# The sigmoid of a projected group, issued later by a fiber of its own, in the last block of a hybrid decoder layer's input projection

## The chip, the cores and the metric

The kernel runs on one core of a Trainium2 chip. The engines of that core work through queues of their own, each in order: PE (TensorE, matrix products into PSUM), DVE (VectorE), ACT (ScalarE), POOL (GpSimd) and SP (SyncE, which here issues the transfers from memory). They wait for each other through semaphores. The metric is the time of one execution in microseconds (us), lower is better; several executions are timed and their median is given.

## The reference

The layer takes x (256 tokens of 4096 channels) and a condition vector c. Cut to what matters here:

```python
mod = c @ w_ada + b_ada                       # shift, scale, gate: 3 x 4096
u = x * (1.0 + scale) + shift
proj = u @ w_in                               # 4096 -> 11824 columns
(rg_x, rg_g, nsa_q, kv_c, kv_s, kv_w, nsa_gl, nsa_g,
 hg_q, hg_f, hg_i, hg_g) = split(proj)
y_rg  = rg_lru(conv(rg_x)) * silu(rg_g)       # gated linear recurrence
y_nsa = nsa(nsa_q, kv_c, kv_s, kv_w, nsa_gl) * silu(nsa_g)   # sparse attention
y_hg  = hgrn2(silu(hg_q), hg_f, hg_i) * silu(hg_g)           # chunked recurrence
y = concat([y_rg, y_nsa, y_hg]) @ w_out
x = layer_norm(ALPHA * x + (1.0 + gate) * y)
```

silu(a) is a * sigmoid(a). Four of the twelve parts pass through it: rg_g, hg_q, hg_g and nsa_g, together 20 groups of 256 columns. All is float32.

## The kernel before, in words

**The projection.** w_in is read once, in ten blocks of rows (KB gives their sizes; the last five are 4 x 128 rows each). A block is walked as a row of steps, one for about 1024 columns of weights in SBUF: in the last block a step is mostly one group of 256 output columns, 24 matmuls. The groups come in the order of GROUPS: kc, vc, four rg_g, four rg_x, four hg_q, four hg_g, hg_f and hg_i in turn, ks, one nsa_q, kw, vw, eight nsa_g, seven nsa_q, vs. Each group has a sum `acc` in SBUF (ACC) over the ten blocks.

**A step.** Weights are split in a rounded part `hi` and a remainder `lo`, so that three fast matmuls make one float32 product. `split` issues, three steps ahead of the matmuls, on ACT the casts `hi` (1024 wide) and `ps` (a second copy of half of it in PSUM), on POOL one half of `lo`, on DVE the other half. There are four raw, four hi and four lo buffers. In program order a step is: the split of the step three further on; the loads; the first half of the matmuls; `post` of the step before (which empties PSUM: DVE adds `mm` to `acc`); one turn of the background work; the second half of the matmuls; another turn of the background work; then `ease` and `ada_loads`, which issue on DVE the sums of a chunk of the gate matrix w_ada (two instructions `ps<-ra,pk,ps`). The line L119 that most profile rows show is the helper through which DVE, ACT and POOL instructions are issued, so rows are told apart by their tiles.

**The last block.** Here `post` does more (the lines inside `if kb == NKB - 1`): for a group in SILU it issues at once, behind the DVE addition, a sigmoid on ACT into a buffer `ev` (two buffers) and a multiplication of `acc` by `ev` on POOL; then the group is entered in `done`. Between the last block's steps stand 16 steps of another kind (cmp), which compress keys and values: a few small matmuls each on weights `ra` from w1, and no split.

**Background work.** The three head groups are generators ("fibers") on lanes: rg_fiber, hg_fiber, nsa_fiber. They start when the groups they need are in `done` and buffers suffice. `run_bg` makes a turn: it counts one tick, gives every entry of the list `fibers` a go, then every lane. `advance` lets a fiber run to its next yield if its due tick has come, and sets the next due tick from what the planner thinks the engines owe. That estimate is the class Meter: each engine has a ledger `owed`, to which an instruction adds a fixed part and a part per column (DVE 0.06 + 0.00104 per column, ACT 0.09 + 0.00084, POOL 0.16 + 0.0021; ACT also 1.3 when the function table changes), and from which 1.28 (HALF) is taken in each turn. In the last block a step has two turns. Lanes stand still while the ledger of DVE or ACT is over 2.5 (MAY_OWE); the list `fibers` doesn't. An rg_fiber uses sigmoid and tanh, then exp, then sqrt, and so changes ACT's function table on its way; an hg_fiber uses sigmoid, and sqrt near its end.

The order of the program is thus fixed when the kernel is built, and each engine follows its own part of it.

Of the kernel before, what the change touches and what calls it, by code (L numbers as in the profile page):

```python
# [11 lines left out]
FT = mybir.dt.float32  # L12
FR = mybir.dt.float32r
I32 = mybir.dt.int32
AF = mybir.ActivationFunctionType
# [3 lines left out]
P = 128  # L19
# [37 lines left out]
def chunks(kb):  # L57

    n, out, cur, o = KB[kb], [], [], 0
    for g in GROUPS:  # L60
        m = max(1, min(n, 1024 // g[3]))
        for a in range(0, n, m):
            b = min(n, a + m)
            if o + (b - a) * g[3] > 1024:
                out.append((cur, o))
                cur, o = [], 0
            cur.append((g, a, b, o))
            o += (b - a) * g[3]
    out.append((cur, o))
    return out  # L70
# [64 lines left out]
def trunk(ctx: ExitStack, tc: tile.TileContext, pack, xT, xz, w_ada, b_row, w_in, w_out, rg_w, w1, w2,  # L135
          ln_gb, out):
    nc = tc.nc
    dve = Meter(nc.vector, 0.06, 0.00104)
    act = Meter(nc.scalar, 0.09, 0.00084)
    pool = Meter(nc.gpsimd, 0.16, 0.0021)  # L140
# [3 lines left out]
    strm = ctx.enter_context(tc.tile_pool(name="strm", bufs=1))  # L144
# [7 lines left out]
    def nm(s):  # L152
        cnt[0] += 1
        return f"{s}_{cnt[0]}"
# [6 lines left out]
    def slot(name, shape, dt=FT):  # L161
        used[0] += 1
        return ring.tile(shape, dt, name=nm(name), tag="slot", bufs=NRING)

    def ps_mm():
        return psum.tile([P, 512], FT, name=nm("mm"), tag="ps", bufs=8)
# [177 lines left out]
    cur, tick = [0], [0]  # L344
# [78 lines left out]
    ACC = {}  # L423
    done = set()
# [3 lines left out]
    for kb in range(NKB):  # L428
        state = {}
        for items, width in chunks(kb):  # L430
            st = Step("win", off, width)
            st.kb = kb
            off += P * width
            steps.append(st)
            for g, a, b, o in items:

                def mm(st=st, g=g, a=a, b=b, o=o, kb=kb, state=state):
                    name, i, _, w, lay = g
                    k0 = KB0[kb] + a
                    hi, lo = (t_[:, o:o + (b - a) * w].rearrange("p (k w) -> p k w", w=w) for t_ in (st.hi, st.lo))  # L440
                    if a == 0:
                        state[name, i] = [ps_mm() for _ in range(2 if w > 256 else 1)]
                    ps = state[name, i]
                    for j in range(2):
                        dst = ps[j][:, :w] if w > 256 else ps[0][:, j * 256:(j + 1) * 256]
                        for k in range(b - a):
                            uh, ul = U[k0 + k]
                            s, e = a + k == 0, a + k == KB[kb] - 1
                            if lay == "nt":
                                wh, wl = hi[:, k, j * P:(j + 1) * P], lo[:, k, j * P:(j + 1) * P]  # L450
                                seq = ((wh, uh), (wh, ul), (wl, uh))
                            else:
                                wh, wl = hi[:, k], lo[:, k]
                                uh, ul = uh[:, j * P:(j + 1) * P], ul[:, j * P:(j + 1) * P]
                                seq = ((uh, wh), (uh, wl), (ul, wh))
                            for n_, (l_, r_) in enumerate(seq):
                                nc.tensor.matmul(dst, lhsT=l_, rhs=r_, start=s and n_ == 0, stop=e and n_ == 2)  # L457
                        yield

                def post(g=g, b=b, kb=kb, state=state):  # L460
                    if b < KB[kb]:
                        return
                    name, i, _, w, _ = g
                    key = (name, i)
                    ps = state.pop(key)
                    if kb == 0:
                        ACC[key] = slot("acc", [P, 2, 256])
                    acc = ACC[key]
                    if w > 256:
                        pairs = [(x_, ps[j][:, c0:c1]) for j in range(2)  # L470
                                 for x_, c0, c1 in ((acc[:, j], 0, 256), (gl[:, j], 256, 304))]
                    else:
                        pairs = [(acc.rearrange("p a b -> p (a b)"), ps[0])]
                    n_post[0] += 1
                    for x_, p_ in pairs:
                        if kb == 0:
                            act.copy(x_, p_)
                        elif w == 256 and n_post[0] % EVAC[KB[kb]] == EVAC[KB[kb]] - 1:
                            t_ = strm.tile([P, 512], FT, name=nm("ev"), tag="ev", bufs=2)
                            act.copy(t_, p_)  # L480
                            pool.tensor_add(x_, t_, x_)
                        else:
                            dve.tensor_add(x_, p_, x_)
                    if kb == NKB - 1:
                        if name in SILU:
                            t_ = strm.tile([P, 2, 256], FT, name=nm("ev"), tag="ev", bufs=2)
                            act.activation(t_, acc, AF.Sigmoid)
                            pool.tensor_mul(acc, acc, t_)
                        done.add(key)

                st.work.append((mm, post))
    n_win = len(steps)
    first_of = {}
    for i, st in enumerate(steps):
# [5 lines left out]
    def cmp_step(which, c):  # L500
# [21 lines left out]
        def post():  # L522
# [11 lines left out]
            done.add(("cmp_h", which))  # L534

        st.work.append((mm, post))
        return st

# [409 lines left out]
    for pi, part in enumerate(PARTS):  # L948
        for nb in range(NB):
            state = {}  # L950
            for ci, pr in enumerate(part):
# [26 lines left out]
                def post(x, pi=pi, nb=nb, ci=ci, state=state, part=part, between=None):  # L978
# [22 lines left out]
                    else:  # L1001
                        dve.tensor_add(z, ps, z)

                st.work.append((mm, post))
                wout_steps.append(st)

# [58 lines left out]
    fibers = []  # L1065
# [265 lines left out]
HALF = 1.28  # L1331
AFTER = (0.2, 1.5)
# [70 lines left out]
```

## Time and profile before

| what | value |
|---|---|
| median of 3 runs | 1662.71 us (1659.02 to 1663.55) |
| the profiled execution's own time | 1660.88 us |
| its span, from first to last instruction | 1659.1 us |
| PE busy, share of the span | 1597.9 us, 96% |
| DVE | 1331.8 us, 80% |
| ACT | 971.6 us, 59% |
| POOL | 954.5 us, 58% |
| mean granted clock of PE | 0.99 |

The shares are averages over the whole span; the last block of the projection lies between about 955 and 1170 us. The first of the 20 sigmoids starts at 966.69 us and the last at 1133.33 us.

### The profile page before, as it was taken

The page shows a single profiled execution, that of the slowest core. Times are in us where ns is not written, and L with a number is a line of the kernel's source. Part 1 is how long each engine was busy: PE and PEld are TensorE (multiplying, and loading weights), DVE is VectorE, ACT ScalarE, POOL GpSimd, SP SyncE. Part 2 cuts the span into 40 slices and gives each one's busy share as a digit, 9 for nine tenths or more (in the row PEclk, how much of TensorE's full clock was granted, in tenths as well). Part 3 has the DMA queues.
Part 4 walks back from the last instruction along what each step waited for, and adds up shares of the span by engine and source line. Part 5 has one row for each costly group of instructions (what it writes and reads, how often), then busy time and mean ns, then how long its engine had stood idle before and what let it go on. Part 6 is the DMA issues. An engine that isn't in the chain of part 4 may idle for free.

```text
span 1659.1 us, 33161 instructions
## 1 busy us (share of the span) xinstructions
PE 1597.9 (96%) x11752; PEld 1497.6 (90%) x11752; DVE 1331.8 (80%) x2301; ACT 971.6 (59%) x1557; POOL 954.5 (58%) x765
## 2 busy tenths in 40 slices
PE   4999999999999999999999999889999999999997
PEld 4999999998999999999999998889888888878884
DVE  5668978799788788788787797899689688968875
ACT  2887666665655555555555566763565566656562
POOL 1579987776655455555455446576453445455655
PEclk9999999999999999999999998999999999999998
DMA  7998989999999899899899886767667766689983
GB/s 287 368 344 313 365 292 343 309 370 327 328 351 334 289 347 327 299 351 327 303 333 332 312 300 223 247 230 266 230 230 242 238 204 215 222 296 374 338 318 126
DMA packets 146486, 491.49 MB, mean 296 GB/s; under 512 B 16264, under 2 KB 17288, under 8 KB 146320
## 3 DMA queue, kind: packets, MB, share of 16 engines
q1 hardware_dynamic: 146320, 489.38, 82.5%
q8 instruction: 92, 1.51, 0.4%
q14 instruction: 74, 0.61, 0.1%
HBM read 485.12 MB, written 4.19 MB: 295 GB/s over the span
## 4 chain that ended last, share of the span: by engine, by line
PE 79%; DVE 11%; DMA 3%; issue 3%; ACT 3%; POOL 0%; SPq 0%; DVEq 0%; ACTq 0%
PE mm L457 50%; PE mm L969 21%; DVE ps L119 3%; DVE acc L119 2%; DVE lo L119 2%; DMA ra<-in_w_ada_dram 1%; ACT hi L119 1%; DMA raw<-in_w_in_dram 1%; PE ps L708 1%; DVE rgt L119 1%; PE ps L901 1%; PE ps L1287 1%; DVE rgy L119 1%; PE ps L792 1%; PE ps L395 1%
## 5 line engine op out<-in xcount | busy, mean ns | idle before, releaser
L119 POOL TENSOR_TENSOR lo<-raw,hi 128x576 fp32r<-128x576 f32 (+4 forms) x527 | 707.7, 1344 | 609.3 <-ACT hi L119 588.4
L119 ACT CAST hi<-raw 128x1024 fp32r<-128x1024 f32 (+3 forms) x527 | 529.1, 1004 | 487.3 <-POOL lo L119 220.4
L457 PE MATMUL mm<-uh,hi 128*128 128x256 f32 x2560 | 719.3, 281 | 15.3 <-DVE lo L119 9.2
L457 PE MATMUL mm<-uh,lo 128*128 128x256 f32 x2560 | 714.0, 279 | 1.9 <-DVE lo L119 1.4
L457 PE MATMUL mm<-ul,hi 128*128 128x256 f32 x2560 | 713.6, 279 | 0.0
L119 DVE SCALAR_TENSOR_TENSOR ps<-ra,pk,ps 128x512 f32<-128x512 f32 x744 | 520.8, 728 | 8.7 <-DMA ra<-in_w_ada_dram 2.9
L457 PEld LDWEIGHTS mm<-uh,hi 128*128 128x128 f32 x2560 | 485.3, 190 | 19.0 <-DVE lo L119 11.8
L457 PEld LDWEIGHTS mm<-uh,lo 128*128 128x128 f32 x2560 | 485.1, 189 | 2.6 <-DVE lo L119 1.9
L457 PEld LDWEIGHTS mm<-ul,hi 128*128 128x128 f32 x2560 | 485.6, 190 | 0.3 <-issue 0.2
L119 DVE TENSOR_TENSOR lo<-raw,ps 128x448 fp32r<-128x448 f32 (+4 forms) x500 | 303.2, 607 | 224.3 <-ACT ps L119 182.6
L119 ACT CAST ps<-raw 128x448 fp32r<-128x448 f32 (+4 forms) x500 | 259.5, 519 | 7.2 <-DVE acc L119 6.5
L119 DVE TENSOR_TENSOR acc<-mm,acc 128x512 f32<-128x512 f32 (+1 forms) x346 | 231.5, 670 | 0.0
L969 PE MATMUL mm<-hi,yh 128*128 128x512 f32 x512 | 210.8, 412 | 0.3 <-ACT ev L119 0.3
L969 PE MATMUL mm<-hi,yl 128*128 128x512 f32 x512 | 201.3, 393 | 0.0
L969 PE MATMUL mm<-lo,yh 128*128 128x512 f32 x512 | 200.1, 391 | 0.0
L969 PEld LDWEIGHTS mm<-hi,yh 128*128 128x128 f32 x512 | 96.4, 188 | 23.4 <-issue 5.7
L969 PEld LDWEIGHTS mm<-hi,yl 128*128 128x128 f32 x512 | 96.1, 188 | 21.6
L457 PE MATMUL mm<-hi,uh 128*128 128x256 f32 (+1 forms) x384 | 110.6, 288 | 4.9 <-ACT hi L119 3.0
L969 PEld LDWEIGHTS mm<-lo,yh 128*128 128x128 f32 x512 | 96.5, 188 | 19.1 <-issue 1.2
L457 PE MATMUL mm<-lo,uh 128*128 128x256 f32 (+1 forms) x384 | 108.9, 284 | 0.0
L457 PE MATMUL mm<-hi,ul 128*128 128x256 f32 (+1 forms) x384 | 108.9, 284 | 0.0
L119 POOL TENSOR_TENSOR acc<-ev,acc 128x512 f32<-128x512 f32 x77 | 101.2, 1315 | 2.8 <-ACT ev L119 2.5
(193 smaller groups left out, 1480.0 us busy)
## 6 DMA issues: line engine op xcount, KB each, us to landing
ra<-in_w_ada_dram SPq DMA_DIRECT2D x323, 512.0 KB, 5.8
raw<-in_w_in_dram SPq DMA_DIRECT2D x291, 512.0 KB, 5.1
raw<-in_w_out_dram SPq DMA_DIRECT2D x128, 512.0 KB, 4.6
raw<-in_w_in_dram SPq DMA_DIRECT2D x90, 384.0 KB, 5.2
ra<-in_w_ada_dram SPq DMA_DIRECT2D x64, 384.0 KB, 5.5
ra<-in_w_dram SPq DMA_DIRECT2D x16, 512.0 KB, 3.9
raw<-in_w_ada_dram SPq DMA_DIRECT2D x13, 512.0 KB, 5.6
xz<-in_xz_dram SPq DMA_DIRECT2D x16, 256.0 KB, 6.0
```

The costliest lines, as they stand in the source:

```text
L119: return f(*a, **k)
L395: nc.tensor.matmul(pp[:, q:q + 1], lhsT=acc[q], rhs=ones[:, 0:1], start=kb > 0, stop=True, skip_group_check=kb == 0)
L457: nc.tensor.matmul(dst, lhsT=l_, rhs=r_, start=s and n_ == 0, stop=e and n_ == 2)
L708: nc.tensor.matmul(pl[:, (2 * x + j) * 64:(2 * x + j + 1) * 64], lhsT=k[:, j, x * P:(x + 1) * P], rhs=qp[:, j, x * P:(x + 1) * P].rearrang ...
L792: nc.tensor.matmul(s1[:, b * T:(b + 1) * T], lhsT=q[:, j, P:], rhs=kk[b][:, g], start=True, stop=True)
L901: nc.tensor.matmul(o, lhsT=v0, rhs=eT[:, 0:2], start=b == 0, stop=False)
L969: nc.tensor.matmul(state[x], lhsT=a_, rhs=b_, start=ci == 0 and j == 0 and n_ == 0, stop=ci == len(part) - 1 and j == 1 and n_ == 2)
L1287: nc.tensor.matmul(pb, lhsT=rows[-1 - x], rhs=rows[i // 2][:, i % 2 * 512:i % 2 * 512 + 512], start=True, stop=True)
```

## The change

The branch for groups in SILU no longer issues the sigmoid and the multiplication itself. It puts a new generator `silu(key)` on the list `fibers`, with a due tick that depends on the ledgers of DVE and POOL at that moment. When its tick has come, the fiber issues the same two instructions on the same tiles and enters the group in `done`. AFTER[1] is 1.5. Groups outside SILU are entered in `done` at once, as before.

```diff
                     if kb == NKB - 1:
                         if name in SILU:
-                            t_ = strm.tile([P, 2, 256], FT, name=nm("ev"), tag="ev", bufs=2)
-                            act.activation(t_, acc, AF.Sigmoid)
-                            pool.tensor_mul(acc, acc, t_)
-                        done.add(key)
+                            owed = max(dve.owed, pool.owed)
+                            fibers.append([silu(key), 0, 0, 0, tick[0] + 1 + math.ceil((owed + AFTER[1]) / HALF)])
+                        else:
+                            done.add(key)
 
                 st.work.append((mm, post))
+    def silu(key):
+
+        acc = ACC[key]
+        t_ = strm.tile([P, 2, 256], FT, name=nm("ev"), tag="ev", bufs=2)
+        act.activation(t_, acc, AF.Sigmoid)
+        pool.tensor_mul(acc, acc, t_)
+        done.add(key)
+        yield 0
+
```

## Rows read from the trace of the kernel before

**Rows 1.** The page: busy time and share; the chain that ended last, by engine.
```profile
PE 1597.9 (96%) x11752; PEld 1497.6 (90%) x11752; DVE 1331.8 (80%) x2301; ACT 971.6 (59%) x1557; POOL 954.5 (58%) x765
...
PE 79%; DVE 11%; DMA 3%; issue 3%; ACT 3%; POOL 0%; SPq 0%; DVEq 0%; ACTq 0%
```

**Rows 2.** Busy time of each engine in four stretches.
```profile
core 0: us, PE busy (x) PEld busy (x) DVE busy (x) ACT busy (x) POOL busy (x), PEclk, DMA share, GB/s
961.00:1012.00 51.00, 50.77 (x425) 50.03 (x425) 40.67 (x64) 36.35 (x56) 27.03 (x21) 1.00 0.78 277
1012.00:1021.00 9.00, 6.94 (x34) 6.74 (x34) 6.79 (x11) 4.82 (x7) 3.32 (x3) 0.63 0.61 215
1021.00:1060.00 39.00, 32.41 (x229) 30.43 (x228) 38.41 (x54) 19.37 (x32) 25.80 (x19) 0.91 0.68 240
1085.00:1141.00 56.00, 49.27 (x402) 47.75 (x401) 55.46 (x86) 29.75 (x46) 45.36 (x38) 0.97 0.72 248
```

**Rows 3.** The chain, 955 to 1160 us, shares by line.
```profile
by line: issue 11.9%; DVE acc L119 11.0%; PE mm L457 8.8%; DVE lo L119 8.6%; DVE ps L119 7.5%; DVE rgt L119 7.4%; DVE rgy L119 6.5%; DVE hgA L119 5.3%; ACT hi L119 4.9%; DVE hgqp L119 3.3%; PE ps L708 3.1%; DMA raw<-in_w_in_dram 2.8%; ACT p
```

**Rows 4.** Waits, 940 to 1200 us: total us, times, longest.
```profile
ACT ev L119 <- DVE acc L119: 41.3, 14, 7.8
POOL acc L119 <- ACT ev L119: 31.0, 15, 8.9
...
ACT L119 <- DVE acc L119: 3.5, 1, 3.5
...
ACT ev L119 <- POOL acc L119: 2.8, 2, 1.4
```

**Rows 5.** DVE groups in 961:1021, then 1021:1060: busy, mean ns, idle before.
```profile
L119 DVE TENSOR_TENSOR lo<-raw,ps 128x512 fp32r<-128x512 f32 x13 | 8.9, 683 | 10.0 <-ACT ps L119 7.8 <-POOL acc L119 2.2
...
L119 DVE TENSOR_TENSOR lo<-raw,ps 128x512 fp32r<-128x512 f32 x9 | 6.1, 680 | 2.0 <-ACT ps L119 2.0
```

**Rows 6.** Timeline of ACT, 994 to 1020 us: start, duration, idle before.
```profile
993.98 0.90 ACT L119 ACTIVATE rgt<-rgr,p 128x256 f32<-128x256 f32 x2
996.18 0.63 ACT L119 ACTIVATE ev<-acc 128x512 f32<-128x512 f32 x1 [1.30 <-DVE acc L119]
...
1004.68 1.28 ACT L119 ACT_TABLE_LOAD   x1
1006.02 0.63 ACT L119 ACTIVATE ev<-acc 128x512 f32<-128x512 f32 x1
1006.55 1.04 ACT L119 CAST hi<-raw 128x1024 fp32r<-128x1024 f32 x1
...
1012.90 0.58 ACT L119 CAST ps<-raw 128x512 fp32r<-128x512 f32 x1
1016.94 1.28 ACT L119 ACT_TABLE_LOAD   x1 [3.46 <-DVE acc L119]
...
1018.77 1.03 ACT L119 CAST hi<-raw 128x1024 fp32r<-128x1024 f32 x1
```

**Rows 7.** Timeline of DVE, 1000 to 1021 us.
```profile
1000.55 0.69 DVE L119 TENSOR_TENSOR lo<-raw,ps 128x512 fp32r<-128x512 f32 x1 [2.94 <-ACT ps L119]
...
1008.10 0.69 DVE L119 TENSOR_TENSOR lo<-raw,ps 128x512 fp32r<-128x512 f32 x1 [2.12 <-ACT ps L119]
...
1020.32 0.69 DVE L119 TENSOR_TENSOR lo<-raw,ps 128x512 fp32r<-128x512 f32 x1 [2.00 <-ACT ps L119]
```

**Rows 8.** PE's wait in 1012:1060; SP's issue of the weights it waited for.
```profile
PE ps L511 <- DMA ra<-in_w_dram: 2.1, 1, 2.1
...
1010.87 0.33 SPq L1032 DMA_DIRECT2D ra<-in_w_dram  x1
```

**Rows 9.** Timelines of DVE (two scans of one shape) and of POOL, 1033 to 1042 us.
```profile
1033.19 1.26 DVE L119 TENSOR_TENSOR_SCAN rgt<-rgr,rgi 128x256 f32<-128x256 f32 x2
...
1038.51 3.34 DVE L119 TENSOR_TENSOR_SCAN rgt<-rgr,rgi 128x256 f32<-128x256 f32 x2
...
1038.20 1.50 POOL L119 TENSOR_TENSOR acc<-acc,ev 128x512 f32<-128x512 f32 x1
```

## The prediction, as it went on record

> **What bounds the kernel now.** I read first the page. PE is busy for 96% of the span and holds 79% of the chain that ended last [rows 1], so over the whole kernel only time in which PE waits can be won. The change touches nothing outside the last block, so I looked next at the busy times by stretch there [rows 2]. In 961 to 1012 PE works 50.77 of 51 us. From 1012 on it doesn't: 6.94 of 9, 32.41 of 39 and, later, 49.27 of 56 us, and in the same stretches the granted clock is 0.63, 0.91 and 0.97, so part of the work ran at 1.2 GHz in place of 2.4. DVE meanwhile goes from 40.67 of 51 to 38.41 of 39 and 55.46 of 56. The chain of this part says the same: between 955 and 1160 the matmuls of the projection have 8.8% of it, and most of the rest is DVE's [rows 3]. So here DVE's queue sets the time, and PE fills in. A saving in this block is worth what it takes out of DVE's queue or of DVE's idle time inside that chain, not what it takes from ACT.
>
> The waits name what the change is about [rows 4]. ACT stood still 41.3 us, 14 times, in front of a sigmoid whose sum DVE hadn't made, 2.8 us more where the profile names POOL, and 3.5 us in front of a table load for such a sigmoid: 47.6 us in all. POOL stood 31.0 us in front of the multiplications. That is large, but ACT and POOL are not the chain. The question is where ACT, standing there, holds back a cast that DVE then waits for. DVE's groups answer: in 961 to 1021 the subtractions `lo<-raw,ps` had 10.0 us of idle time before them, 7.8 of it on ACT's cast `ps`; in 1021 to 1060 only the 2.0 us at 1020.32, which this window counts again [rows 5]. From 1085 to 1141 DVE has 0.5 us free in all [rows 2].
>
> **What is removed.** Two places count, both at ACT's table changes among the rg fibers.
>
> First place: the two tanh end at 993.98 + 0.90 = 994.88. ACT waits 1.30 us for the sum of hg_q0, does the sigmoid, loads tables for exp and for sqrt, does two splits between them, loads the sigmoid's table (1.28) and does the next sigmoid at 1006.02, before the cast `hi` at 1006.55 [rows 6]. That is 11.67 us. DVE idles twice for it, 2.94 and 2.12 us [rows 7].
>
> Now the order with the fiber. The due tick is the present one + 1 + ceil((owed + 1.5) / 1.28). At the first twelve sigmoids the larger ledger, followed through the steps of the kernel before by its own constants, stands between 0.6 (the sum alone: 0.06 + 0.00104 x 512) and 3.1 (that sum, a split's half, a chunk of 1.19, and what is left over): 3 to 5 ticks. A step has two. So one or two splits get ahead of each sigmoid. The sigmoid of hg_q0 lands behind the second exp and in front of the first sqrt, that of hg_q1 behind that sqrt. Up to the cast at 1006.55 there are still three table loads (exp, sigmoid, sqrt in place of exp, sqrt, sigmoid). The wait of 1.30 goes, and one sigmoid (1006.55 - 1006.02 = 0.53) is no longer in front. So the cast starts 1.83 us earlier, and with it DVE's subtraction at 1008.10.
>
> Second place: after the cast `ps` at 1012.90 + 0.58 = 1013.48 ACT waits 3.46 us, loads the table and does a sigmoid, and only at 1018.77 comes the next `hi` [rows 6]. DVE idles 2.00 us for it [rows 7]. With the fiber that split stands in front of the sigmoid; its casts end before 1016, so DVE goes on without the gap: 2.00 us. Between the two places DVE's queue is full, so the terms add: 1.83 + 2.00 = 3.83 us.
>
> **What I count as nothing.** The other idle time of DVE in 961 to 1021 (10.0 - 2.94 - 2.12 - 2.00, about 2.9 us [rows 5, 7]) lies before 980, while PE worked without a wait [rows 2]: PE's matmuls and DVE's later wait of 2.94 us cover it. If that cover is gone it is worth up to 2.9 us. The wait of PE at 1012 for weights of a cmp step, 2.1 us, shrinks: SP issued them at 1010.87, behind a chunk sum on DVE that moves up by the 1.83 [rows 8]; but PE isn't the chain, so it adds nothing unless DVE catches up. The sigmoids of 1021 to 1060 and of nsa_g: DVE is full there, ACT's waits (the longest 7.8) cost nothing and removing them gives nothing. For nsa_g POOL's ledger is higher, 2.5 to 7, so these wait 5 to 8 ticks, but their users start later than that.
>
> **What is added or moved.** The same 20 sigmoids (0.63) and 20 multiplications; no transfer. One table load more: hg_q1's sigmoid now stands between the two sqrt with hg_q2's, and hg_q0's already needed one. The 1.28 falls where ACT has slack before DVE's full queue (1008.8 to 1018.3), so nothing; without that cover 1.28. What stands behind the moved sigmoid on ACT is the next split, but 3 to 5 ticks have passed by then, some 4 to 7 us at the step time below, so the wait for the sum is near zero; the bound is the longest wait of now, 7.8. The planner's ledger for ACT rises above 2.5 when the sigmoid comes between exp and sqrt, which holds the rg lanes back a tick or two, and hg fibers start behind them; one tick is half a step. It costs nothing as long as w_out's first steps have other work; its bound is two ticks, one step's 24 matmuls (about 2.7 us from 50.77 us for 425 matmuls, 0.12 us each).
>
> The multiplications move on POOL against DVE's work, and this is what I can't place. A scan takes 1.26 us for two in one place and 3.34 in another, where POOL was doing one of these multiplications and one of the rg fiber's [rows 9]: 2.1 us more. Per multiplication (1.50) I bound the effect by plus or minus 1.0 us, and take zero for the sum, since POOL runs much else beside DVE now.
> The Trainium skill (SBUF — State Buffer, "Who interferes with whom") states that a VectorE instruction with two SBUF inputs contends with a GpSimd instruction that reads SBUF, and that one of the two blocks. The two scans agree with it. By that rule it decides which DVE instructions the multiplications now fall on: today they follow a sum that reads PSUM, later they come beside the fibers' work in SBUF, which speaks against the change.
>
> **The sum.** Profiled execution: 1660.88 - 3.83 = 1657.05 us. That execution lies 1.83 below the median of the runs, so against the median: 1662.71 - 3.83 = 1658.9 us.
>
> **The rivals.**
> *More than that (1654.8).* The multiplications leave the crowded places: the one at 1038.20 lay on the scan of 3.34. If it and the one before it go elsewhere, DVE's full stretch shrinks by 2.1 + 2 x 1.0 = 4.1 us beside the 3.83: 1662.71 - 7.9. For it: 0.59 us free of 39 there, so each microsecond shows. Against it: POOL's own rg multiplications stay beside the scan. With the 2.9 us counted as nothing above, the end is 1652.
> *Nothing (1662.7).* What DVE wins by 1021 is given back: the rg lanes held back two ticks bring hg fibers and with them a wait of w_out, or the same queue of DVE simply meets the same PE stalls. For it: PE is nowhere 3.8 us late before 1012.
> *Slower (1668).* In 1085 to 1141 DVE has 0.5 us free [rows 2]. Eight nsa_g multiplications and two of hg_g come 3 to 4 steps later, among hg's products of two SBUF tiles. At 1.0 us a collision, nine or ten more cost 9 to 10 us: 1658.9 + 9.5 = 1668.4. It decides from nine on: four more give back the 3.83, five beyond these are 0.3%. Against it: POOL is busy 45.36 of 56 already, so most of those products collide now.
>
> **Chances and range.** About 0.3% (5 us) is what a measurement of this kernel can tell from no change. My forecast, 3.8 us faster, 0.45; more than that 0.27; nothing 0.13; slower 0.15. The forecast's own range is 1656 to 1661.5, which lies mostly inside the 5 us: I give 0.09 of its 0.45 to faster. Faster is then 0.26 + 0.09 = 0.35, slower 0.14 (0.01 of that case stays inside), no measurable change 0.51. The range that leaves 2 in 10 out goes from 1651 (below the larger gain's 1652) to 1667 (nearly the slower rival's 1668.4).
>
> **What would show it.** Right: ACT's waits for `acc` before `ev` fall from 47.6 to under 15 us; POOL's for `ev` from 31.0 to under 12; the idle time before `lo<-raw,ps` in 961 to 1021 from 10.0 to about 6 or less; PE's wait for cmp weights at 1012 below 0.5 us; table loads one more. The end of the last block comes some 4 us earlier, and all behind it keeps that distance. Wrong: if DVE's busy time in the block grows by several microseconds with the same instructions (collisions), if table loads grow by three or more with splits behind them, or if PE's idle time returns in the first steps of w_out.

## The result

The changed kernel is slower: 1674.22 us median (1667.65 to 1675.64) against 1663.13 us for the kernel before on the same chip, ratio 1.0059 [1.0037, 1.0081]. One of the four executions behind the 1663.13 was in a slower state of the chip (1788.52 us); the ratios here and below leave such executions out, and without it the median is 1662.71. A second measurement gave 1.0045 [1.0026, 1.0063]. The forecast was 1658.9 us, and the range ended at 1667. The profiled execution took 1667.65 us, span 1665.8, mean granted clock 0.993.

### The profile page after: what moved, and what is told of

Read it like the earlier page. It is cut to its first block, busy times and chain, and to the rows that moved or that the text cites. A ratio compares the mean times of both kernels' runs of the same rounds, so it can differ in the third digit from the quotient of the medians.

```text
span 1665.8 us, 33152 instructions
## 1 busy us (share of the span) xinstructions
PE 1595.2 (96%) x11752; PEld 1493.2 (90%) x11752; DVE 1335.3 (80%) x2301; ACT 976.5 (59%) x1559; POOL 954.7 (57%) x765
```

## The profile after

The same views as before, of the changed kernel. First the page: busy time, share of the span and instructions of each engine; it answers to [rows 1].

```profile
PE 1595.2 (96%) x11752; PEld 1493.2 (90%) x11752; DVE 1335.3 (80%) x2301; ACT 976.5 (59%) x1559; POOL 954.7 (57%) x765
```

Nothing in it tells where 6.7 us of span went: PE does the same matmuls, and the shares are the same but for POOL's, 57% in place of 58%. The stretches do. Busy time of each engine (PE, PEld, DVE, ACT, POOL), granted clock, share of DMA, as in [rows 2]:

```profile
961.00:1012.00 51.00, 51.00 (x430) 50.58 (x429) 43.72 (x67) 39.52 (x60) 26.96 (x21) 1.00 0.81 294
1012.00:1021.00 9.00, 8.88 (x78) 8.67 (x76) 8.80 (x13) 8.15 (x12) 7.86 (x7) 1.00 0.62 231
1021.00:1060.00 39.00, 31.48 (x224) 29.91 (x224) 37.69 (x54) 20.28 (x37) 22.61 (x17) 0.91 0.69 252
1085.00:1141.00 56.00, 48.71 (x391) 47.05 (x392) 55.46 (x87) 28.40 (x43) 40.85 (x35) 0.97 0.75 254
```

In 1012 to 1021 PE works 8.88 of 9 us at full clock, where it worked 6.94 at 0.63. In 1085 to 1141 DVE is busy 55.46 us, to the digit what it was. So PE lost less at the second of the places that the forecast named. From 1021 to 1060 it works 31.48 us in place of 32.41; the wait of 4.6 us in the next list lies there. The waits from 940 to 1200 us, against [rows 4] (total, times, longest):

```profile
ACT ev L119 <- DVE acc L119: 13.1, 8, 5.7
...
POOL acc L119 <- ACT ev L119: 5.3, 7, 1.1
...
PE ps L520 <- DMA ra<-in_w_dram: 4.6, 1, 4.6
...
ACT ev L119 <- POOL acc L119: 1.4, 1, 1.4
```

ACT's wait before the sigmoids fell from 47.6 to 14.5 us (13.1, and 1.4 on POOL), POOL's from 31.0 to 5.3. The idle time before DVE's subtractions in 961 to 1021, then in 1021 to 1060, against [rows 5]:

```profile
L119 DVE TENSOR_TENSOR lo<-raw,ps 128x512 fp32r<-128x512 f32 x13 | 8.9, 683 | 5.6 <-ACT ps L119 5.4 <-issue 0.2
...
L119 DVE TENSOR_TENSOR lo<-raw,ps 128x512 fp32r<-128x512 f32 x9 | 6.1, 675 | 0.0
```

And the timeline of ACT that answers to [rows 6] (start, duration, idle before):

```profile
999.56 1.28 ACT L119 ACT_TABLE_LOAD   x1
1000.85 0.63 ACT L119 ACTIVATE ev<-acc 128x512 f32<-128x512 f32 x1
...
1004.76 1.03 ACT L119 CAST hi<-raw 128x1024 fp32r<-128x1024 f32 x1
...
1012.90 0.63 ACT L119 ACTIVATE ev<-acc 128x512 f32<-128x512 f32 x1
1013.44 1.03 ACT L119 CAST hi<-raw 128x1024 fp32r<-128x1024 f32 x1
```

The forecast put the first cast at 1006.55 - 1.83 = 1004.72; it starts at 1004.76. In the second place the cast that started at 1018.77 before starts at 1013.44. It stands behind the sigmoid of 1012.90, and neither that sigmoid nor its table load had to wait. From its first matmul to w_out's first, the last block takes 206.8 us (957.14 to 1163.94) in place of 213.6 (956.49 to 1170.11).

The loss lies behind it. Busy time of PE (with its matmuls), clock and DMA in 1175 to 1630 us, nearly all of w_out, first of the kernel before:

```profile
1175.00:1630.00 455.00, 453.73 (x2220) 1.00 0.73 257
```

then of the changed kernel:

```profile
1175.00:1630.00 455.00, 446.23 (x2173) 1.00 0.74 253
```

PE idled 1.27 us in these 455 us and now idles 8.77. The waits of PE there, changed kernel:

```profile
PE ps L896 <- DVE e L119: 2.2, 1, 2.2
PE ps L910 <- DVE lo L119: 1.8, 1, 1.8
PE ps L742 <- POOL hgk L119: 1.6, 1, 1.6
PE mm L978 <- POOL lo L119: 0.9, 2, 0.6
PE mm L978 <- ACT z L119: 0.8, 1, 0.8
PE ps L802 <- DVE lo L119: 0.8, 1, 0.8
PE ps L896 <- DVE lo L119: 0.6, 1, 0.6
```

They are eight small ones in seven rows, on three engines, in fibers (e, hgk), in splits (lo) and in w_out's own ends (z). No sigmoid that the change touches is near: the last of the 20 is long over. What differs here is only the order in which the planner issued the fibers and what stands beside them. Their start ticks (the first tick in which each fiber issues something), read off the planner:

```
            before                            after
rg 3, 4     761 762                           764 765
hg          776 788 792 852                   768 792 800 851
nsa         860 868 876 917 925 933 952 960   863 870 877 918 926 934 958 966
```

How such a wait arises can be read at the longest, 1370.55 to 1372.77. DVE in the changed kernel:

```profile
1366.17 1.45 DVE L119 TENSOR_SCALAR e<-e,sm 128x128 f32<-128x128 f32 x4
...
1368.17 1.54 DVE L119 SCALAR_TENSOR_TENSOR ps<-ra,pk,ps 128x512 f32<-128x512 f32 x2
1369.62 0.68 DVE L119 TENSOR_TENSOR lo<-raw,ps 128x512 fp32r<-128x512 f32 x1
1370.21 1.90 DVE L119 TENSOR_SCALAR e<-e,sm 128x128 f32<-128x128 f32 x4
1372.04 1.00 DVE L119 SCALAR_TENSOR_TENSOR e<-dist,ps 128x512 f32<-128x512 f32 x2
```

No gap stands between these rows: DVE's queue is full. PE's next transposes wait by their semaphore for the first of the two `e<-dist,ps`, which empties a buffer in PSUM; it ends at 1372.71, and PE goes on at 1372.77. In front of it stand a chunk sum of the gate matrix, a split and the scaling of `e`. That scaling takes 1.90 us, beside POOL's half of a split (1370.04 to 1371.31). In the kernel before it takes 1.00, with no POOL instruction beside it:

```profile
1367.99 1.00 DVE L119 TENSOR_SCALAR e<-e,sm 128x128 f32<-128x128 f32 x4
```

So part of this wait is the place in the queue, and up to 0.9 us of it may be that overlap; no run separates the two. One more wait, in w_out's last part: here the end of the gate (`gate<-ps,gate`) comes directly in front of the end of a step. DVE:

```profile
1557.16 0.69 DVE L119 SCALAR_TENSOR_TENSOR gate<-ps,gate 128x512 f32<-128x512 f32 x1 [4.81 <-DMA gate<-in_b_row_dram]
```

and POOL:

```profile
1560.72 1.30 POOL L119 TENSOR_TENSOR z<-z,gb 128x512 f32<-128x512 f32 x1 [8.27 <-DMA raw<-in_w_out_dram]
1561.97 1.29 POOL L119 TENSOR_TENSOR lo<-raw,hi 128x512 fp32r<-128x512 f32 x1
```

DVE waits 4.81 us for a row of the bias that the end of the gate loads. The kernel before has that wait too, but three splits earlier in DVE's queue, 6.1 us in front of the step's end, and there PE doesn't wait:

```profile
1543.96 0.69 DVE L119 SCALAR_TENSOR_TENSOR gate<-ps,gate 128x512 f32<-128x512 f32 x1 [3.98 <-DMA gate<-in_b_row_dram]
```

In the changed kernel POOL's product needs the `z` that DVE makes after it (the profile puts POOL's wait down to a transfer of raw weights), so POOL's half of the split comes late, and PE's two waits on POOL's `lo` in the list above are those behind it.

## The experiments

**Theory A**: the moved sigmoids win as forecast, and the planner's new order loses more than that in w_out. **Theory B**: the order is worth nothing, and the moved instructions themselves cost (POOL's multiplications on DVE, the sigmoids' place on ACT). The change does two things that can be done apart: it issues 40 instructions later, and it charges the planner's ledgers for them later (and enters the group in `done` later). The edits below are cut to what matters: `...` marks a cut, the text behind a # is mine, `issue` issues the sigmoid and the multiplication without telling the ledgers, and `charge` adds their cost to the ledgers.

**1. Only the instructions moved.** The charge and the entry stay where they were, so every other instruction keeps its place in the order of before (the programs of PE, DVE and SP are those of the kernel before, instruction by instruction).

```diff
...
-                            act.activation(t_, acc, AF.Sigmoid)
-                            pool.tensor_mul(acc, acc, t_)
+                            owed = max(dve.owed, pool.owed)
+                            moved.append((tick[0] + 1 + math.ceil((owed + AFTER[1]) / HALF), key))
+                            charge()          # the ledgers, at once
                         done.add(key)
...
+        while moved and moved[0][0] <= tick[0]:
+            issue(moved.pop(0)[1])            # the two instructions, unmetered
```

> The sigmoids and multiplications are issued as many ticks later as in the change, but the planner's ledgers are charged, and the group is entered in done, where the kernel before did it; so every other instruction keeps the order of before on every engine. Theory A (the sigmoids' move wins some 4 to 6 us in the last block as forecast, and the loss comes from the other instructions' new order behind it): 1656 to 1660 us, 0.2 to 0.4% faster than before, and the first steps of w_out some 4 us earlier. Theory B (the move itself costs, through collisions of POOL's multiplications with DVE): 1667 to 1675 us.

Measured: 0.9961 [0.994, 0.9982], faster than both kernels.

**2. Only the order.** The two instructions at once, the charge and the entry by the fiber. PE, DVE and SP then have the changed kernel's programs.

```diff
+                            issue(key)
                             owed = max(dve.owed, pool.owed)
                             fibers.append([silu(key), ...])
...
     def silu(key):
...
-        act.activation(t_, acc, AF.Sigmoid)
-        pool.tensor_mul(acc, acc, t_)
+        charge()
         done.add(key)
```

> The reverse: the sigmoids and multiplications are issued at once as before, but the planner is charged, and the groups enter done, at the later tick; so all other instructions have exactly the changed kernel's order. Theory A: at least as slow as the changed kernel, 1672 to 1680 us. Theory B: like the kernel before, within 3 us of 1663.

Measured: 1.0091 [1.0072, 1.0109].

**3. The changed kernel, once more beside these two.**

> The changed kernel itself, timed beside the two others on one chip, and profiled once more since its profiled execution (1667.65) was the fastest of four. Both theories: 1667 to 1676 us. If the slower executions lose time in places where the profiled one did not, this profile shows them: theory A expects these in the steps of w_out, theory B between 1020 and 1145 us.

Measured: 1.0045 [1.0026, 1.0063]. The halves multiply to 0.9961 x 1.0091 = 1.0052, between the two measurements of the whole (1.0059, 1.0045). Theory A holds, B falls: the move wins 0.39%, the order loses 0.91%. PE's busy time in 1175 to 1630, first of the kernel with the move alone, then of the one with the order alone:

```profile
1175.00:1630.00 455.00, 453.74 (x2203) 1.00 0.74 256
```

```profile
1175.00:1630.00 455.00, 446.19 (x2187) 1.00 0.73 254
```

The first is nearly that of the kernel before (453.73), the second nearly that of the changed kernel (446.23).

**4. The move in parts, order kept**: the twelve sigmoids of rg_g, hg_q and hg_g; the eight of nsa_g; the four of hg_q.

```diff
+                            if name == "nsa_g":       # the eight: name != "nsa_g"; the four: name != "hg_q"
+                                moved.pop()
+                                issue(key)
                             charge()
```

> The twelve sigmoids of rg_g, hg_q and hg_g are issued later, nsa_g at once, and all other instructions keep the order of before. By the prediction's sum the gain lies at the table changes of the first two rg fibers: 3 to 9 us faster than before, about as fast as the kernel with all twenty moved. If POOL's later multiplications of nsa_g were what helps: like before.

> Only the eight sigmoids of nsa_g are issued later, all else in the order of before. By the prediction (DVE is full there, so nothing): within 3 us of before. By its slower rival (collisions of the multiplications with DVE): 5 to 10 us slower.

> As the kernel with the sigmoids moved and every other instruction in its old order, but for the four groups of hg_q alone; rg_g, hg_g and nsa_g stay at once. If the gain of the move lies at the two places that the prediction named (ACT between 994 and 1020 us, where the sigmoids of hg_q stand among the table changes), all of it is here: 0.9963, as with twelve moved, by the prediction's own terms 0.9977 (3.83 us). If the gain lies with the sigmoids of rg_g or hg_g, in POOL's multiplications for one, 0.999 to 1.001.

Measured: twelve 0.9963 [0.995, 0.9976]; eight 1.0011 [0.9998, 1.0023]; four 0.9978 [0.9961, 0.9995]. The nsa_g part gives nothing that can be told from noise. The four of hg_q, which stand among ACT's table changes, give 0.0022 x 1662 = 3.7 us (0.8 to 6.5 by the interval), by the prediction's terms 3.83. The twelve give 6.1 us; that the other eight of them add 2.4 us isn't shown, the intervals overlap. It would fit the idle time before DVE's subtractions ahead of 980 us that the prediction counted as nothing: 2.96 us before (0.72 + 2.24), as much with the four moved, 0.39 with the twelve.

**5. The change for the twelve alone**, nsa_g at once: a cheap cure, if nsa_g's later charge were the trouble.

```diff
-                        if name in SILU:
+                        if name == "nsa_g":
+                            ...                       # as before the change
+                        elif name in SILU:
                             owed = max(dve.owed, pool.owed)
```

> The change for rg_g, hg_q and hg_g alone; the eight nsa_g keep sigmoid and multiplication at once, as before. The order behind the block comes out almost as in the changed kernel. Theory A (the twelve sigmoids' charges in the ledgers shift the rg and hg fibers, and with them w_out's neighbours): 1667 to 1675 us. Theory C (what costs is the lateness of the eight nsa_g): 1656 to 1661 us.

Measured: 1.0069 [1.0045, 1.0092]. It isn't: all fibers start at the ticks of the changed kernel, and the time is again that of the changed kernel.

**6. Other orders, no sigmoid moved.** The threshold at which lanes stand still, in the kernel before:

```diff
-MAY_OWE = 2.5
+MAY_OWE = 2.6
```

> The kernel before with MAY_OWE 2.6 in place of 2.5: all sigmoids at once, but the planner comes to another order of the fibers, on PE close to that of the changed kernel (nsa fibers start 1 to 6 ticks later). Theory A (that order costs, whatever brought it about): 8 to 16 us slower than before. If the cost needs the moved sigmoids: like before, within 4 us.

Measured: 1.0071 [1.0053, 1.0089]. On PE this order is near the changed kernel's (at least 10816 of the 11124 matmuls keep its sequence), and PE's waits of 2.2 and 1.8 us come back. So a like order costs like that, reached by another way. By its start ticks it is less alike, and other than I expected: rg 761 762, as before; hg 778 786 794 848; nsa 860 866 874 915 923 931 955 963, six of these eight not later than before. Which part of an order costs was asked of three more, all from the kernel before: nsa fibers held back to the ticks of the changed kernel or later (they start at 864 874 882 919 927 935 959 967); rg fibers 3 and 4 held back (they start at 765 and 766, one tick later than in the changed kernel); and one constant of the ledger changed.

```diff
             while len(busy) < LANES[n] and lane and ...:
+                if HOLD.get((n, len(lane)), 0) > tick[0]:
+                    break
...
+HOLD = {(2, 8): 863, (2, 7): 870, ...}        # nsa;  rg: {(0, 2): 764, (0, 1): 765}
```

```diff
-    act = Meter(nc.scalar, 0.09, 0.00084)
+    act = Meter(nc.scalar, 0.08, 0.00084)
```

> The kernel before, sigmoids at once, with one hold: an nsa fiber may not start before the tick at which it starts in the changed kernel (863, 870, 877, 918, 926, 934, 958, 966). The rg and hg fibers start as before (761, 762; 776, 788, 792, 852), the nsa fibers at 864, 874, 882, 919, 927, 935, 959, 967. Theory N, that the order costs because the nsa units come later in w_out: 1.006 to 1.010, and the waits of PE seen at 1370 and 1464 us in the changed kernel, 2.2 and 1.8 us, come back. Theory R, that it costs because rg fibers 3 and 4 fall behind the first hg fiber: 0.998 to 1.002 and none of these waits. Theory T, that any order but the tuned one costs: also slower, by 1.003 or more.

> The kernel before, sigmoids at once, with one hold: the rg fibers 3 and 4 may not start before ticks 764 and 765, those of the changed kernel, in place of 761 and 762. By the planner's own doing the first hg fiber then starts at 768 in place of 776 and the second at 792, as in the changed kernel, the third at 794, and the nsa fibers at 859, 863, 908, 915 and so on, up to nine ticks earlier than before in the middle. Theory R, that the swap of rg and hg costs: 1.006 to 1.010. Theory N, that the later nsa units cost: no slower than 1.002. Theory T, any other order costs: 1.003 or more.

> The kernel before with one constant of the planner changed, ACT's fixed part 0.08 in place of 0.09 us; sigmoids at once. The rg fibers start as before, hg at 778, 786, 794, 849, nsa at 857, 865, 873, 914, 922, 930, 951, 961, so nearly all earlier by one to three ticks. Theory N: 0.997 to 1.002. Theory R: the same, for the first hg fiber doesn't pass the rg fibers. Theory T, that the order before is a tuned one and any other costs: 1.003 or more.

Measured: nsa held 1.0052 [1.0032, 1.0073]; rg held 1.0073 [1.0048, 1.0098]; lighter ledger 1.0077 [1.0049, 1.0105]. Theory T (any other order costs) stands: each of the three costs. Theory N (the later nsa fibers cost) alone falls with the lighter ledger, where seven of eight nsa fibers start earlier; of the two waits that it wanted back with nsa held, the one of 1.8 us came and the one of 2.2 didn't. Theory R (the rg fibers behind the first hg fiber cost) alone falls with nsa held and with the lighter ledger, where the rg fibers start as before. The kernel with rg held tells less of N than I expected: fiber by fiber its third nsa goes from 876 to 908, which I had read as a fourth one moved up. PE in 1175 to 1630, nsa held, rg held, lighter ledger:

```profile
1175.00:1630.00 455.00, 450.32 (x2205) 1.00 0.75 258
```

```profile
1175.00:1630.00 455.00, 447.41 (x2182) 1.00 0.73 256
```

```profile
1175.00:1630.00 455.00, 449.27 (x2187) 1.00 0.75 257
```

And each order has waits of its own. PE's in that stretch with the rg fibers held, beside the list of the changed kernel above:

```profile
PE ps L887 <- DVE e L119: 2.1, 2, 1.7
PE ps L793 <- DVE lo L119: 1.8, 2, 0.9
PE mm L969 <- DVE lc L119: 1.8, 2, 1.4
PE ps L733 <- POOL hgk L119: 1.2, 1, 1.2
```

All runs, by PE's idle time in those 455 us:

| kernel | order of fibers | ratio to before | PE idle, 1175 to 1630 |
|---|---|---|---|
| before | before | 1 | 1.3 |
| all moved, order kept | before | 0.9961 | 1.3 |
| twelve moved | before | 0.9963 | 1.8 |
| eight moved | before | 1.0011 | 1.3 |
| four moved | before | 0.9978 | 1.3 |
| nsa held | own | 1.0052 | 4.7 |
| lighter ledger | own | 1.0077 | 5.7 |
| rg held | own | 1.0073 | 7.6 |
| threshold 2.6 | own, on PE near the changed one's | 1.0071 | 7.8 |
| order only | changed | 1.0091 | 8.8 |
| changed | changed | 1.0059, 1.0045 | 8.8, 9.2 |
| twelve by fiber | changed, by start ticks | 1.0069 | 9.3 |

Every kernel with the old order idles under 2 us, every other one 4.7 or more, whether sigmoids were moved or not. The time of all of w_out sorts them the same way: from its first matmul to its last it takes 461.6 to 463.2 us in the five profiles with the old order and 468.1 to 478.1 in the others. PE over that time, kernel before, then order only:

```profile
1170.11:1631.74 461.63, 460.36 (x2254) 1.00 0.73 256
```

```profile
1173.48:1648.90 475.42, 465.58 (x2269) 1.00 0.72 250
```

## Why the prediction was wrong

**The step that failed** is the one on the planner's ledger, "which holds the rg lanes back a tick or two, and hg fibers start behind them ... It costs nothing as long as w_out's first steps have other work; its bound is two ticks, one step's 24 matmuls", given as about 2.7 us (24 times its 0.12 is 2.9). The first half of the event was rightly seen (three ticks, 761 to 764, where I had two). The second was not: the first hg fiber doesn't start later, it starts earlier, at 768 in place of 776. The price was wrong, and so was the reason for the bound. It counted the delay where it arises. But the order is fixed when the kernel is built, and every later start follows from the ledgers and the starts ahead of it: holding these two fibers alone (to 765 and 766) brings the first hg fiber forward from 776 to 768 and puts the third nsa fiber off from 876 to 908. That one edit, no sigmoid moved, measured 1.0073: 12.1 us where the bound said 2.7. The whole order measured 1.0091, 15.1 us. In the planner it is the late charge that does it: with the groups entered in `done` late and the charge at once, all fibers start at the ticks of before; with the charge alone late they start at those of the changed kernel. I named ACT's ledger; with ACT's charge alone late the rg fibers start at 760 and 764 and the first hg fiber at 769, with POOL's alone late at 762 and 764 and at 768. So each has a part. These orders were read off the planner, not timed.

**The sum of 3.83 us** was right in place and, as far as its parts can be read, in size: the cast starts at 1004.76, DVE's subtraction behind it at 1006.31 in place of 1008.10, the wait of 2.00 us at the second place is gone, and hg_q alone measured 0.9978. At the second place the order came out otherwise than forecast, with the sigmoid still in front of the cast. That the subtractions' idle time is 5.6, where I said about 6, is luck. DVE at the first place, changed kernel:

```profile
998.78 0.69 DVE L119 TENSOR_TENSOR lo<-raw,ps 128x512 fp32r<-128x512 f32 x1 [1.66 <-ACT ps L119]
...
1003.00 0.69 DVE L119 TENSOR_TENSOR lo<-raw,ps 128x512 fp32r<-128x512 f32 x1 [3.52 <-ACT ps L119]
```

These two come to 5.18 us where there were 5.06. What fell beside the second place is the 2.96 us ahead of 980, to 0.40, and this I had counted as nothing. In the kernel with the move alone the same group of 961 to 1021 reads

```profile
L119 DVE TENSOR_TENSOR lo<-raw,ps 128x512 fp32r<-128x512 f32 x12 | 8.2, 684 | 3.1 <-ACT ps L119 2.8 <-issue 0.2
```

Its two places together went from 7.06 to 2.66 us, and the idle time ahead of 980 from 2.96 to 0.39. With the order kept, the move beats the kernel before by 6.5 us (0.39% of 1662; the interval is 3.0 to 10.0), between the forecast and the rival *More*. The sum with the term counted as nothing would be 3.83 + 2.6 = 6.4; the interval is too wide to show that this is what it lacked. Nor does the last block's own time show it: in the five profiles with the old order it reads 206.3 to 218.0 us.

**The gain by collisions gone (*More*)** isn't seen where it was argued. The scan that took 3.34 us takes 3.39 with the multiplications moved [rows 9]. DVE, then POOL:

```profile
1032.12 1.26 DVE L119 TENSOR_TENSOR_SCAN rgt<-rgr,rgi 128x256 f32<-128x256 f32 x2
...
1034.73 3.39 DVE L119 TENSOR_TENSOR_SCAN rgt<-rgr,rgi 128x256 f32<-128x256 f32 x2
```

```profile
1033.46 1.28 POOL L119 TENSOR_TENSOR rgt<-rgt,acc 128x512 f32<-128x512 f32 x1 [4.77 <-DVE rgt L119]
1034.70 1.26 POOL L119 TENSOR_TENSOR acc<-acc,ev 128x512 f32<-128x512 f32 x1
1035.93 1.64 POOL L119 TENSOR_TENSOR lo<-raw,hi 128x512 fp32r<-128x512 f32 x1
```

Another multiplication came to stand there. The scans of 1.26 us ran while POOL waited 4.77 us, those of 3.39 beside two of POOL's instructions on SBUF tiles. This agrees once more with the rule of the Trainium skill that the prediction cited (SBUF — State Buffer, "Who interferes with whom").

***Nothing*** had the mechanism, "rg lanes held back two ticks bring hg fibers and with them a wait of w_out", and as its price the gain of the forecast; the price was four times that. ***Slower*** had the sign and nearly the time (1668.4; measured 1674.22 and 1670.55), by luck, for its mechanism was wrong: the nsa_g multiplications cost at most 0.2% where it had 0.6% (1.0011 [0.9998, 1.0023]), and DVE's busy time in 1085 to 1141 stayed at 55.46.

**Signs.** ACT's waits under 15 (14.5), POOL's under 12 (5.3), the idle time (5.6): right. PE's wait for cmp weights at 1012 went, as said, but one of 4.6 us came at 1034, not foreseen: SP issued the weights at 1034.85, after 3.4 us of waiting for a chunk sum on DVE that ended at 1034.82. Table loads: one more was forecast, 18 became 22, and three or more was a sign of being wrong. With the order kept they are 19, so the forecast held for the order that it assumed; with the order alone they are 22 too. That "all behind it keeps that distance" is false: at the first step of w_out the changed kernel was 6.2 us ahead, at its last step 9.5 us behind. Wrong "if PE's idle time returns in the first steps of w_out": it returned in all three parts of it, so the prediction's own sign for the failed step came out.

**What stays open.** Between the profiles of the kernel before and of the order alone, w_out grows from 461.6 to 475.4 us, by 13.8, close to the 15 that the order costs. PE's idle time is 8.6 of these (9.84 in place of 1.27), and a lower clock 1.7 (3.4 us at 1.2 GHz in place of none). In the other 3.5 PE is busy, in part with the fibers: in the program 16 of their small matmuls, which stood ahead of the projection's last matmul, stand behind it now, 8 of them ahead of w_out's first. What these 16 cost no run separates. In the changed kernel w_out takes 477.3 us; the last block's 6.8 us less are set against 15.6 more there. Nor was a rule found by which one could tell a good order: that the old one beats the five others timed without a moved sigmoid may come from the planner's constants having been chosen for it, which is argued, not shown. Which of an order's waits costs how much is open too; each was read, none was removed by itself.

## What to carry to other kernels

When a kernel's order is written by a planner, an edit has two prices: what its instructions do, and what the planner does with every instruction behind them. Charge the ledgers as before and let only the instructions move, and the first price stands alone: here 0.9961 instead of 1.0059. And a gain of 4 us in a kernel whose PE is 96% busy should be weighed against the spread of orders: five edits of planning alone, no sigmoid moved, made this one slower by 0.5 to 0.9%.

## What the runs showed of the hardware

The same wait of 2.2 us, before the same matmul, had two consequences. In both cases PE had run at full clock and without a gap for 10 us before. In the changed kernel's profile (busy time of PE, clock, DMA):

```profile
1370.60:1372.70 2.10, 0.00 (x0) 1.00 0.84 275
1373.20:1376.40 3.20, 3.20 (x12) 0.50 0.44 118
```

and in the second profile of that kernel:

```profile
1371.60:1373.70 2.10, 0.00 (x0) 1.00 0.92 289
1374.20:1377.40 3.20, 3.20 (x20) 1.00 0.34 91
```

PE was granted 1.2 GHz for the 3.2 us behind the wait in the one (12 matmuls) and 2.4 GHz in the other (20), with the same busy time and the same program. Three more kernels here have this wait. Behind it PE ran at 1.2 GHz with the threshold 2.6 and with the twelve by fiber, and at 2.4 GHz with the order alone. So a wait of this length cost its own 2.2 us, and in three of five profiles about half of the next 3.2 us more.
